# Softmax over rows on one core: three stores of 32 rows per partition in place of six of 16, and the scaling dealt out anew

## The chip, the core and the metric

The kernel runs on one core of one Trainium2 chip. The metric is the device time of one execution in microseconds. Before the change it is 160.23 us, the median of three runs (160.09 to 160.33).

The engines that matter here: VectorE (DVE in the profile), ScalarE (ACT), GpSimd (POOL), and SyncE (SP), which computes nothing and issues every transfer. The transfers run on 16 DMA engines, all fed through SP's one hardware queue.

## The reference

```python
def reference(x):                       # x: 16 x 1024 x 512, float32
    x_max = np.max(x, axis=-1, keepdims=True)
    exp_x = np.exp(x - x_max)
    return (exp_x / np.sum(exp_x, axis=-1, keepdims=True)).astype(np.float32)
```

There are 16,384 rows of 512 numbers, 2 KB each. 33.6 MB have to be read and as many written.

## The kernel before

The rows are flattened to 16,384 and cut into eight chunks of 4 MB. Each of the 128 partitions holds 16 successive rows of a chunk, so 32 KB lie together per partition both in DRAM and on the chip. The buffer `held` (line 79) has six places of 16 rows per partition. Chunks 6 and 7 therefore go into the places of chunks 0 and 1, once those have been stored. Everything is done in place: load, exponential, scaling, store.

Compute goes by groups of 8 rows per partition, two to a chunk, 16 in all. A group passes through four steps:

- M: `reduce_max` on VectorE (line 133) writes the negated row maxima into `shift`.
- exp: eight activations on ScalarE (line 165), one per row of the group, write the exponential in place and the row's sum into `sums`.
- the reciprocal of the sums on VectorE (line 142).
- the scaling, one `tensor_mul` of 128 x 4096 numbers with the reciprocals broadcast (line 144). It runs on VectorE for groups 12 to 15 (`ON_VECTOR`) and on GpSimd for the others. In the text, P5 is the scaling of group 5 on GpSimd, V14 that of group 14 on VectorE, M14 and exp 14 the other steps.

Each engine works through its instructions in the order in which they are written, and waits at semaphores. `take` (line 92) waits until a semaphore has reached a number and subtracts it. Four orders, written out by hand, make the schedule.

SP's order is the list `ORDER`: loads 0 to 5, stores 0, 1, 2, loads 6 and 7, stores 3 to 7. The first six loads wait for nothing (line 112), and the first of these is moved ahead of the start barrier by `loads_at_the_head`. A store waits for both scalings of its chunk, and load 6 or 7 waits until store 0 or 1 has landed:

```python
if what == "L":
    ...
        take(nc.sync, stored[k - PLACES], 16)
        ...
    nc.sync.dma_start(out=place(k), in_=x_rows[k]).then_inc(loaded[k], 16)
else:
    take(nc.sync, scaled[k], PER)
    nc.sync.dma_start(out=out_rows[k], in_=place(k)).then_inc(stored[k], 16)
```

VectorE's order is M0, M1, then by turns the reciprocal of group g - 1 (with its scaling, where that is VectorE's) and M of group g + 1, up to the scaling of group 15. The first M of a chunk waits for the chunk's load. ScalarE runs two loops with the same body, twelve turns for groups 0 to 11 and four for groups 12 to 15, because the second starts again at the first place of `held`. A turn waits for one count of `maxed`. GpSimd runs its twelve scalings in the order of the groups.

Of the kernel before, what the change touches and what calls it, by code (L numbers as in the profile page):

```python
# [1 line left out]

# [4 lines left out]

F32 = mybir.dt.float32
EXP = mybir.ActivationFunctionType.Exp
AX = mybir.AxisListType.X  # L10

CHUNK = 16
CHUNKS = 8
PLACES = 6
GROUP = 8
PER = CHUNK // GROUP
GROUPS = CHUNKS * PER
RING = PLACES * PER  # L20


ORDER = [("L", k) for k in range(PLACES)] + [
    ("S", 0),
    ("S", 1),
    ("S", 2),
    ("L", 6),
    ("L", 7),
    ("S", 3),
    ("S", 4),  # L30
    ("S", 5),
    ("S", 6),
    ("S", 7),
]


ON_VECTOR = (12, 13, 14, 15)


AT_HEAD = {mybir.EngineType.SP: 1}  # L40

def loads_at_the_head(nc):

    main, body = nc.main_func.blocks[0], nc.main_func.blocks[1]
    for engine, count in AT_HEAD.items():
        loads = [
            i
            for i in body.instructions  # L50
            if i.engine == engine and type(i).__name__ == "InstDMACopy"
        ][:count]
        barrier = next(
            n
            for n, i in enumerate(main.instructions)
            if i.engine == engine and type(i).__name__ == "InstDrain"
        )
        for load in loads:
            body.instructions.remove(load)
        main.instructions[barrier:barrier] = loads  # L60


@with_exitstack
def kernel(
    ctx: ExitStack,
    tc: tile.TileContext,
    x: bass.AP,
    out: bass.AP,
):
    nc = tc.nc  # L70
    nc.at_finalize(loads_at_the_head)
    P = nc.NUM_PARTITIONS

    x_rows = x.flatten_outer_dims().rearrange("(c p r) d -> c p r d", p=P, r=CHUNK)
    out_rows = out.flatten_outer_dims().rearrange("(c p r) d -> c p r d", p=P, r=CHUNK)
    n, _, _, d = x_rows.shape
    assert n == CHUNKS

    held = nc.alloc_sbuf_tensor("held", [P, PLACES * CHUNK, d], F32).ap()
    shift = nc.alloc_sbuf_tensor("shift", [P, GROUPS * GROUP], F32).ap()  # L80
    sums = nc.alloc_sbuf_tensor("sums", [P, GROUPS * GROUP], F32).ap()
    recip = nc.alloc_sbuf_tensor("recip", [P, GROUPS * GROUP], F32).ap()

    loaded = [nc.alloc_semaphore(f"loaded{k}") for k in range(CHUNKS)]
    stored = [nc.alloc_semaphore(f"stored{k}") for k in range(CHUNKS)]
    maxed = nc.alloc_semaphore("maxed")
    expd = nc.alloc_semaphore("expd")
    to_pool = nc.alloc_semaphore("to_pool")
    to_vector = nc.alloc_semaphore("to_vector")
    scaled = [nc.alloc_semaphore(f"scaled{k}") for k in range(CHUNKS)]  # L90

    def take(engine, semaphore, n):

        engine.wait_ge(semaphore, n).then_inc(semaphore, -n)  # L94

    def place(k):
        at = (k % PLACES) * CHUNK
        return held[:, at : at + CHUNK, :]

    def rows(g):  # L100
        at = (g % RING) * GROUP
        return held[:, at : at + GROUP, :]

    def stats(t, g):
        return t[:, g * GROUP : (g + 1) * GROUP]

    with tc.manual_schedule():  # L110
        for _, k in ORDER[:PLACES]:
            first = nc.sync.dma_start(out=place(k), in_=x_rows[k])
            first.then_inc(loaded[k], 16)
            tc.no_tile_sem_insts.add(first.ins.name)
    tc.close()
    tc.compile()  # L116

    reused = set()
    for what, k in ORDER[PLACES:]:
        if what == "L":  # L120
            if k >= PLACES:
                take(nc.sync, stored[k - PLACES], 16)
                reused.add(k - PLACES)
            nc.sync.dma_start(out=place(k), in_=x_rows[k]).then_inc(loaded[k], 16)
        else:
            take(nc.sync, scaled[k], PER)
            nc.sync.dma_start(out=out_rows[k], in_=place(k)).then_inc(stored[k], 16)


    def rowmax(g):  # L130
        if g % PER == 0:
            take(nc.vector, loaded[g // PER], 16)
        nc.vector.reduce_max(  # L133
            out=stats(shift, g), in_=rows(g), axis=AX, negate=True
        ).then_inc(maxed, 1)

    def scale(g):
        engine, ready = (
            (nc.vector, to_vector) if g in ON_VECTOR else (nc.gpsimd, to_pool)
        )  # L140
        take(nc.vector, expd, 1)
        nc.vector.reciprocal(out=stats(recip, g), in_=stats(sums, g)).then_inc(ready, 1)  # L142
        take(engine, ready, 1)
        engine.tensor_mul(  # L144
            out=rows(g),
            in0=rows(g),
            in1=stats(recip, g).unsqueeze(2).to_broadcast([P, GROUP, d]),
        ).then_inc(scaled[g // PER], 1)

    for g in range(GROUPS):  # L150
        rowmax(g)
        if g:
            scale(g - 1)
    scale(GROUPS - 1)


    nc.scalar.preload_act_table(EXP)  # L157

    def exps(first, turns):
        with nc.scalar.Fori(0, turns) as i:  # L160
            take(nc.scalar, maxed, 1)
            for r in range(GROUP):
                row = held[:, bass.ds(i * GROUP + r, 1), :]
                at = bass.ds(i * GROUP + (first * GROUP + r), 1)
                act = nc.scalar.activation(  # L165
                    out=row,
                    in_=row,
                    func=EXP,
                    bias=shift[:, at],
                    scale=1.0,  # L170
                    accum_out=sums[:, at],
                )
            act.then_inc(expd, 1)

    exps(0, RING)
    exps(RING, GROUPS - RING)


    for k in range(CHUNKS):
        if k not in reused:  # L180
            take(nc.sync, stored[k], 16)


# [1 line left out]
_INS = ['x']  # L185
_OUTS = [((16, 1024, 512), 'float32')]


# [23 lines left out]
```

## Time and profile before

| | before |
|---|---|
| median of three runs | 160.23 us (160.09 to 160.33) |
| the profiled execution | 160.32 us |
| its span, first to last instruction | 159.0 us |
| moved | 67.13 MB in 2306 packets, 422 GB/s over the span |
| busy: VectorE, ScalarE, GpSimd | 90.6, 92.0, 84.0 us |
| one reduction, one GpSimd scaling, one VectorE scaling (means) | 4.40, 7.02, 4.58 us |
| one activation (mean) | 0.706 us |
| loads, stores | 8 and 8, of 4 MB each |

The profile's page first gives the busy time of each engine, then the span in 40 equal slices, where each digit is the busy share in tenths and the DMA row is the mean share of the 16 DMA engines. After that come the share of the hardware queue, the chain of work that ended last, and the groups of instructions with busy time and mean duration. Beyond the page, the trace can be asked for the instructions of one engine in order of time: start, busy time, engine and line, operation, output and input, count, and in brackets the idle time before with what ended it. For one tile it gives the issues of its transfers in a window, with the duration and start of the issue and the time from issue to landing, each as minimum, median and maximum. All times are microseconds from the start of the span, durations of instructions in such rows nanoseconds.

### The profile page before, as it was taken

Reading aid. Unit: us, or ns where it says so; the run is one execution under the profiler, and the core shown is the slowest. Engines: PE = TensorE matmul, PEld = TensorE weight load, DVE = VectorE, ACT = ScalarE, POOL = GpSimd, SP = SyncE. Lnnn points to the kernel's source line nnn. Section 1 sums busy time; section 2 is a strip of 40 time slices with the busy share of each in tenths; the row PEclk is TensorE's granted clock in tenths of the full one; section 3 lists DMA queues with packets and bytes.
Section 4 is the critical chain, followed back from the end, with each engine's and each line's share of the span. In section 5 each row is a group of like instructions: output and inputs, shape, how many; then the busy total and the mean of one; then the engine's idle time right before and its main releaser. Section 6 shows DMA issues by size and latency. Waiting matters only on the chain. (4 is left out here: it accounts for less than half of the span.)

```text
span 159.0 us, 740 instructions
## 1 busy us (share of the span) xinstructions
DVE 90.6 (57%) x36; ACT 92.0 (58%) x257; POOL 84.0 (53%) x16
## 2 busy tenths in 40 slices
DVE  0008959777977977887700000695999998740000
ACT  0300699999999999999993000059934929200000
POOL 0000009999999999999999999259200000000000
DMA  7999999999999999999999999999999999999995
GB/s 264 470 445 404 404 478 437 396 470 445 404 404 470 445 396 396 396 412 470 437 396 445 470 404 404 478 437 398 437 437 437 412 462 414 437 437 429 429 429 256
DMA packets 2306, 67.13 MB, mean 422 GB/s; under 512 B 256, under 2 KB 256, under 8 KB 256
## 3 DMA queue, kind: packets, MB, share of 16 engines
q1 hardware_dynamic: 2304, 67.11, 98.8%
q14 instruction: 2, 0.02, 0.0%
HBM read 33.55 MB, written 33.55 MB: 422 GB/s over the span
## 5 line engine op out<-in xcount | busy, mean ns | idle before, releaser
L165 ACT ACTIVATE held<-held,shift x128 | 90.3, 706 | 40.0 <-ACTq L94 40.0
L144 POOL TENSOR_TENSOR held<-held,recip 128x4096 f32<-128x4096 f32 x12 | 83.8, 7018 | 28.1 <-POOLq L94 28.1
L133 DVE TENSOR_REDUCE shift<-held 128x8 f32<-128x4096 f32 x16 | 70.3, 4398 | 33.3 <-DVEq L94 33.3
L165 ACT ACTIVATION_READ_ACCUMULATOR held<-held,shift x128 | 23.8, 186 | 0.0
L144 DVE TENSOR_TENSOR held<-held,recip 128x4096 f32<-128x4096 f32 x4 | 18.3, 4576 | 0.6
L142 DVE RECIPROCAL recip<-sums 128x8 f32<-128x8 f32 x16 | 3.2, 201 | 16.4 <-DVEq L94 16.4
L157 ACT ACT_TABLE_LOAD x1 | 1.3, 1283 | 4.0 <-PEq L116 4.0
L196 POOL MEMSET const-float32-0.0<- 128x1 f32 x1 | 0.1, 99 | 0.2 <-issue 0.2
L196 POOL MEMSET const-uint8-127<- 128x1 uint8 x1 | 0.1, 103 | 0.0
L196 POOL MEMSET const-bfloat16-1.0<- 128x1 bf16 x1 | 0.1, 102 | 0.0
L196 POOL MEMSET const-float32-1.0<- 128x1 f32 x1 | 0.1, 99 | 0.0
## 6 DMA issues: line engine op xcount, KB each, us to landing
held<-in_x_dram SPq DMA_DIRECT2D x8, 4096.0 KB, 29.9
out_dram<-held SPq DMA_DIRECT2D x8, 4096.0 KB, 28.3
```

The costliest lines, as they stand in the source:

```text
L133: nc.vector.reduce_max(out=stats(shift, g), in_=rows(g), axis=AX, negate=True).then_inc(maxed, 1)
L142: nc.vector.reciprocal(out=stats(recip, g), in_=stats(sums, g)).then_inc(ready, 1)
L144: engine.tensor_mul(out=rows(g), in0=rows(g), in1=stats(recip, g).unsqueeze(2).to_broadcast([P, GROUP, d]),).then_inc(scaled[g // PER], 1)
L157: nc.scalar.preload_act_table(EXP)
L165: act = nc.scalar.activation(out=row, in_=row, func=EXP, bias=shift[:, at], scale=1.0, accum_out=sums[:, at],)
L196: nc = _bacc.Bacc("TRN2", target_bir_lowering=False, num_devices=1)
```

## The change

The unit is no longer a chunk but a range of rows per partition, of 128 in all. The first two ranges are laid out in DRAM as before, (0,16) and (16,32); the rest in three blocks of 32 rows per partition, so that 64 KB lie together per partition. Loads still bring 16 rows per partition each, now out of a 64 KB stretch from row 32 on. The stores of the three blocks send 32 rows per partition at once, 8 MB each. In SP's order the store of rows 32 to 63 stands ahead of the two late loads. Each store waits for the scaling of each of its groups, now two or four, each with a semaphore of its own.

VectorE's order is written out as a list. M is a reduction; P and V are both the reciprocal, followed by the scaling on GpSimd or on VectorE. GpSimd has 13 scalings instead of 12, and VectorE keeps three, of groups 7, 14 and 15. ScalarE has one loop of 16 turns, in which the place in `held` is the turn's remainder by 12.

```diff
-ORDER = [("L", k) for k in range(PLACES)] + [
-    ("S", 0),
-    ("S", 1),
-    ("S", 2),
-    ("L", 6),
-    ("L", 7),
-    ("S", 3),
-    ("S", 4),
-    ("S", 5),
-    ("S", 6),
-    ("S", 7),
+BLOCKS = [(0, 16), (16, 32), (32, 64), (64, 96), (96, 128)]
+ORDER = [
+    ("L", (0, 16)),
+    ("L", (16, 32)),
+    ("L", (32, 48)),
+    ("L", (48, 64)),
+    ("L", (64, 80)),
+    ("L", (80, 96)),
+    ("S", (0, 16)),
+    ("S", (16, 32)),
+    ("S", (32, 64)),
+    ("L", (96, 112)),
+    ("L", (112, 128)),
+    ("S", (64, 96)),
+    ("S", (96, 128)),
 ]
-ON_VECTOR = (12, 13, 14, 15)
+VECTOR = """
+    M0 M1 P0 M2 P1 M3 P2 M4 P3 M5 P4 M6 P5 M7 P6 M8 V7 M9 P8 M10 P9 M11
+    P10 P11 M12 M13 P12 M14 P13 M15 V14 V15
+"""
...
+    def in_dram(rows, a, b):
+        first, last = next(k for k in BLOCKS if k[0] <= a and b <= k[1])
+        block = rows[first * P : last * P].rearrange("(p r) d -> p r d", p=P)
+        return block[:, a - first : b - first, :]
...
-    for what, k in ORDER[PLACES:]:
+    for what, k in ORDER[AHEAD:]:
         if what == "L":
-            if k >= PLACES:
-                take(nc.sync, stored[k - PLACES], 16)
-                reused.add(k - PLACES)
-            nc.sync.dma_start(out=place(k), in_=x_rows[k]).then_inc(loaded[k], 16)
+            for s in stores:
+                if meets(s, k[0] - RING, k[1] - RING) and s not in taken:
+                    take(nc.sync, stored[s], 16)
+                    taken.add(s)
+            load(k)
         else:
-            take(nc.sync, scaled[k], PER)
-            nc.sync.dma_start(out=out_rows[k], in_=place(k)).then_inc(stored[k], 16)
+            for g in range(GROUPS):
+                if meets(k, *group(g)) and g not in done:
+                    take(nc.sync, scaled[g], 1)
+                    done.add(g)
+            nc.sync.dma_start(out=in_dram(out_rows, *k), in_=rows(*k)).then_inc(
+                stored[k], 16
+            )
...
-    for g in range(GROUPS):
-        rowmax(g)
-        if g:
-            scale(g - 1)
-    scale(GROUPS - 1)
+    for step in VECTOR.split():
+        what, g = step[0], int(step[1:])
+        if what == "M":
+            rowmax(g)
+        elif what == "V":
+            scale(g, nc.vector, to_vector)
+        else:
+            scale(g, nc.gpsimd, to_pool)
...
-        with nc.scalar.Fori(0, turns) as i:
+    with nc.scalar.Fori(0, GROUPS) as i:
...
-                row = held[:, bass.ds(i * GROUP + r, 1), :]
-                at = bass.ds(i * GROUP + (first * GROUP + r), 1)
+            row = held[:, bass.ds(i % (RING // GROUP) * GROUP + r, 1), :]
+            at = bass.ds(i * GROUP + r, 1)
...
-    exps(0, RING)
-    exps(RING, GROUPS - RING)
```

## The prediction

> **What bounds the kernel now.** I read the page first, for what is full, then the landing times of the transfers, then the engines' timelines around the last two loads.
>
> The page, the DMA row of the 40 slices and the row of the one hardware queue:
>
> ```profile
> DVE  0008959777977977887700000695999998740000
> ACT  0300699999999999999993000059934929200000
> POOL 0000009999999999999999999259200000000000
> DMA  7999999999999999999999999999999999999995
> ...
> q1 hardware_dynamic: 2304, 67.11, 98.8%
> ```
>
> The 16 DMA engines are full in every slice but the first and the last, while no compute engine is above 58%. 98.8% of 159.0 us is 157.1 us of transfers; the 1.9 us left are start and tail. So the end is set by the bytes, as long as the queue never runs dry. The question for any change is whether it does.
>
> Next, when each transfer lands (its tile's rows, one window for each issue; the first pair is the first load, then the two late loads, then the last store):
>
> ```profile
> L112 SPq DMA_DIRECT2D held<-in_x_dram x1: 383/383/383, 0.0 to 0.0; - x1
> ...
> DMA to landing us min/median/max: 12.3/12.3/12.3
> ...
> L124 SPq DMA_DIRECT2D held<-in_x_dram x1: 340/340/340, 71.3 to 71.3; - x1
> ...
> DMA to landing us min/median/max: 29.2/29.2/29.2
> ...
> L124 SPq DMA_DIRECT2D held<-in_x_dram x1: 339/339/339, 81.0 to 81.0; - x1
> ...
> DMA to landing us min/median/max: 29.3/29.3/29.3
> ...
> L127 SPq DMA_DIRECT2D out_dram<-held x1: 332/332/332, 141.0 to 141.0; - x1
> ...
> DMA to landing us min/median/max: 17.9/17.9/17.9
> ```
>
> Issue plus time to landing gives 12.3 for load 0, 100.5 for load 6, 110.3 for load 7, 158.9 for store 7. The other rows of the same kind give 61.5 for load 5, then 71.2, 81.0 and 90.8 for stores 0 to 2, and 120.1, 129.8, 139.6 and 149.3 for stores 3 to 6. Everything lands in the order of issue, 9.6 to 9.8 us apart: (158.9 - 12.3) / 15 = **9.77 us for 4 MB**. I use 9.75. The first load met an idle queue and took 12.3, so a transfer that finds the queue empty costs **2.55 us** more than its bytes. Data of the last store ends at 157.2 (the DMA share by microsecond falls there from 1.14 to 0.23), 1.7 before its landing, so a store must have data flowing 1.7 us before the one ahead of it lands. By the bytes moved up to 3.0 us (721 KB, 1.7 us at the mean rate) the first data flows 1.3 us after issue. Together: **a store must be issued 3.0 us before the one ahead lands**, or the queue runs dry. Store 7 was issued at 141.0 and needed by 149.3 - 3.0 = 146.3: a slack of 5.3 us.
>
> **The change, part by part.**
>
> *Order and size on the queue.* The bytes are the same. Stores (0,16) and (16,32) are issued as now (37.7, 51.6) and land at 71.2 and 81.0. Rows 32 to 63 go out as one store of 8 MB ahead of the late loads, two transfers where one stood (store 2): it lands at 81.0 + 19.5 = 100.5, the late loads at 110.25 and 120.0, each 9.75 later than now. Store (64,96) lands at 139.5. Store (96,128), now also 8 MB, needs its issue by 139.5 - 3.0 = **136.5**, 9.8 earlier than store 7 now. Three fewer transfers: the share above leaves no idle time between transfers, so I take nothing; the ends are from a loss to a gain of 0.4 (three times the 0.13 by which the pitch of 9.77 differs from its fastest, about 9.64). That 64 KB lie together per partition in a store, and that late loads step over 64 KB in DRAM, has no row here; 9.75 per 4 MB is the nearest, and I keep 1 us to either side for it.
>
> *Can store (32,64) go out in time?* It needs groups 4 to 7, by 81.0 - 3.0 = 78.0. GpSimd's eleven scalings start at 23.56 and run without a pause (76.77 / 11 = 6.98 each):
>
> ```profile
> 23.56 76.77 POOL L144 TENSOR_TENSOR held<-held,recip 128x4096 f32<-128x4096 f32 x11 [23.12 <-POOLq L94]
> 105.31 7.02 POOL L144 TENSOR_TENSOR held<-held,recip 128x4096 f32<-128x4096 f32 x1 [4.99 <-POOLq L94]
> ```
>
> Groups 0 to 6 on GpSimd end at 23.56 + 7 x 6.98 = 72.4. Group 7 goes to VectorE and could start at 62.9 (its reciprocal is at 62.61 now). But the trace shows what a VectorE scaling does beside a GpSimd one:
>
> ```profile
> 111.58 5.03 DVE L144 TENSOR_TENSOR held<-held,recip 128x4096 f32<-128x4096 f32 x1
> 116.53 4.41 DVE L133 TENSOR_REDUCE shift<-held 128x8 f32<-128x4096 f32 x1
> 120.86 0.18 DVE L142 RECIPROCAL recip<-sums 128x8 f32<-128x8 f32 x1
> 121.19 4.42 DVE L144 TENSOR_TENSOR held<-held,recip 128x4096 f32<-128x4096 f32 x1
> ```
>
> The first one began 0.75 us before GpSimd's last scaling ended (112.33) and took 5.03; the three others met an idle GpSimd and took 4.42. So 0.61 of the 0.75 shared microseconds were lost: while GpSimd scales, VectorE's two-tensor multiply almost stands still. The reductions (4.37 to 4.42 beside GpSimd, 4.41 without) lose nothing. The Trainium skill says the same more strictly ("SBUF — State Buffer", section "SBUF: two separate sides"): the pair of ports that the two engines share is locked for a whole instruction by whichever starts first, and the other blocks fully. By it the 5.03 would be 5.17; the trace is within 0.14 of that.
>
> Whichever goes first, then, the eight scalings follow each other: 72.4 + 4.4 = 76.8, store issued at **77.0**, 1.0 ahead of need. No gap, but thin. If they ran side by side it would be 72.5. Behind the waiting multiply on VectorE stand M9, and P8 to P11; at worst M9 starts at 76.9 instead of 62.7, ScalarE idles meanwhile, and GpSimd runs P8 to P11 from about 81.7 to 109.7. Store (64,96) is needed by 120.0 - 3.0 = 117.0, so this costs nothing. On SP the loads behind the store are issued at about 77.4 and 81.1, far ahead of their turn.
>
> *ScalarE's single loop.* It computes its row address with a remainder; per activation there are two fused register instructions where the first loop had one and an add. The old second loop already had two, and its activations at 105.33, 106.05, 106.76 and 107.46 keep the 0.705 pitch. I cost it at nothing; activations hide it up to 0.7 us per row.
>
> *The end of the chain.* All of it now hangs on load 6, landing at 110.25; M12 starts at 110.35 (100.60 now). With the same distances as now:
> M12 and M13 end at 114.8 and 119.2; exp 12 starts 4.73 after M12 starts (105.33 - 100.60), at 115.1, and exp 13 ends at 126.5. Reciprocal 12 comes 10.63 after M12's start, at 121.0. M14 stands behind it on VectorE, so it runs 121.1 to 125.5 although its load landed at 120.0. P12 on GpSimd starts 0.46 after its reciprocal (as 23.10 to 23.56), 121.4, and ends at 128.5; P13 follows to **135.4**. Reciprocal 13 at 126.5, M15 126.7 to 131.1. Exp 14 follows exp 13 (8 x 0.7055 = 5.64) to 132.1, exp 15 to 137.8. V14 is ready at 132.1 + 0.4 = 132.5, while GpSimd is in P13. If it stands still until 135.4 it ends at 135.4 + 4.3 = 139.7 (4.3, as 112.33 to 116.61); reciprocal 15, then V15 from 140.0 to **144.4**. If the two don't disturb each other, V14 ends at 137.0, V15 starts at 138.2 after exp 15 and ends at 142.6.
>
> SP issues the last store 0.1 later (140.92 to 141.01 now): 144.5, against a need at 136.5. The queue is dry, so the store pays in full: 12.3 + 9.75 = 22.05. It lands at 166.55, and the span ends 0.1 later: **166.65**, 7.65 over 159.0. The profiled execution took 160.32 for its span of 159.0, so 1.32 lie around it, and the median of the runs shown is 0.09 below that execution: 166.65 + 1.32 - 0.09 = **167.9 us**. In short: the last store becomes twice as long, so it must start 9.75 earlier, and its last load lands 9.75 later; 5.3 of slack and a faster finish from load to last scaling (24.4 against 30.6) don't pay for it.
>
> **The rivals.**
> 1. *No standing still of VectorE beside GpSimd* (V14 ends at 137.0): issue 142.7, span 164.85, time 166.1. The 5.03 row speaks against it.
> 2. *Store (32,64) misses its turn.* The cover is 1.0 us. If GpSimd and VectorE lose more than that over group 7, say 2 to 3, the queue is dry by 1 to 2, load 6 is as much later, and all behind it: 169 to 170. The thin margin is for it; against it, that no order of the two gives more than 76.8.
> 3. *The remainder in the loop costs more than the activation hides.* At 0.8 us a row, exp 15 ends at 115.1 + 32 x 0.8 = 140.7, later than V14: V15 then comes 1.1 later than summed, 169.0. At 0.9 it is another 3.2, and exp 7 at 74.8 (17.2 + 64 x 0.9) makes store (32,64) miss as well: 173 to 174. Against it, the pitch of the old second loop.
> 4. *Faster: larger runs move quicker.* The end hangs on the two 8 MB stores ahead of load 6 and at the end, 39 us together. To end before 159.0 they must save 7.7 of it, a rate 1.25 times today's, some 535 GB/s, from which on the change wins; at 1.3 times it gives 158.9. The stretches of 8 to 20 us that I read between 10 and 150 us show 416 to 449 GB/s. The Trainium skill ("DMA: Bandwidth & Descriptors", "Bandwidth") puts the fabric's ceiling at 435 GB/s, which excludes it; the 429 of the pitch agrees.
>
> **How the numbers follow.** Forecast (V14 stands still, no gap earlier) 0.70, 167.9. Rival 1 0.14, rival 2 0.09, rival 3 0.04, rival 4 0.03. The forecast's own bounds are 1 us to either side for the long runs and the idle start, 166.9 to 168.9; the range takes in rival 1 with a margin and the near end of rival 2: 165.6 to 169.3. About 0.2% is what a measurement of this kernel can tell from no change. Faster by more than that 0.02, within it 0.01, slower 0.97.
>
> **What would show it.** Right: GB/s near zero for 5 to 8 us at about 138 to 146; the last store issued near 144.5 and landing 22 us later; the late loads landing near 110 and 120; V14 longer than 6 us, ending 4.3 after P13. Wrong: V14 at 4.4 beside P13 (rival 1); a dip in GB/s near 80 (rival 2); an activation pitch over 0.71 (rival 3); landings less than 18 us apart for an 8 MB store (rival 4). No dip at 138 at all would undo the whole sum.

## The result, and the profile after

The changed kernel takes **166.62 us** (median of five runs, 166.27 to 166.69) against 160.21 us for the kernel before (median of five as well, 160.09 to 160.33): a ratio of 1.0395 with a 95% interval of 1.0383 to 1.0407, slower by 6.4 us. The forecast was 167.9 with a range of 165.6 to 169.3. The profiled span is 165.3 us, 6.3 more than before.

The page of the changed kernel, the rows that answer to those of before:

```profile
DVE  0009957977797788999550000029867789900000
ACT  0200899999999999409999000001999993000000
POOL 0000039999999999999999999200069970000000
DMA  7989999899999989899999969999989991099595
...
q1 hardware_dynamic: 1872, 67.11, 95.1%
```

The transfers fill 95.1% of 165.3 us, which is 157.2, as much as before (157.1). No byte became dearer; the queue had a hole. It stands in slices 34 and 35 of the DMA row (1 and 0). A slice is 4.13 us wide; the issues and landings bound the hole more closely. Rows of the changed kernel's transfers, issue and then time to landing; the two late loads, the store of rows 64 to 95, the last store:

```profile
L123 SPq DMA_DIRECT2D held<-in_x_dram x1: 630/630/630, 77.1 to 77.1; - x1
DMA to landing us min/median/max: 33.2/33.2/33.2
...
L123 SPq DMA_DIRECT2D held<-in_x_dram x1: 340/340/340, 81.1 to 81.1; - x1
DMA to landing us min/median/max: 39.0/39.0/39.0
...
L149 SPq DMA_DIRECT2D out_dram<-held x1: 344/344/344, 104.5 to 104.5; - x1
DMA to landing us min/median/max: 35.3/35.3/35.3
...
L149 SPq DMA_DIRECT2D out_dram<-held x1: 344/344/344, 144.5 to 144.5; - x1
DMA to landing us min/median/max: 20.7/20.7/20.7
```

Rows 0 to 95 are all stored at 139.8 (before: 139.6, store 5). The rest takes 25.4 us now and took 19.3 (158.9 - 139.6). So 6.1 of the 6.3 us lie behind that point. The last store was issued 4.7 us *after* the one ahead had landed, and it took 20.7 us, 1.4 more than the same 8 MB took before. Three windows of the changed kernel (window, length, busy time of each engine, clock, DMA share, GB/s) show what ran in the hole:

```profile
136.00:138.00 2.00, 2.00 (x1) 1.88 (x6) 0.00 (x0) 1.00 0.76 328
138.00:144.90 6.90, 6.29 (x3) 0.00 (x0) 0.00 (x0) 1.00 0.00 1
144.90:165.30 20.40, 0.00 (x0) 0.00 (x0) 0.00 (x0) 1.00 0.95 411
```

Only VectorE works between 138 and 144.9, and no packet of a load or store starts (the 1 GB/s is one packet of 8 KB of the queue that the page calls `instruction`). Its timeline, start and busy time first, shows with what: the first two rows are V7 and the reduction behind it, the last three V14, the reciprocal of group 15 and V15.

```profile
62.82 6.79 DVE L169 TENSOR_TENSOR held<-held,recip 128x4096 f32<-128x4096 f32 x1
69.53 4.41 DVE L161 TENSOR_REDUCE shift<-held 128x8 f32<-128x4096 f32 x1
...
133.14 6.61 DVE L169 TENSOR_TENSOR held<-held,recip 128x4096 f32<-128x4096 f32 x1 [0.56 <-DVEq L107]
139.68 0.19 DVE L167 RECIPROCAL recip<-sums 128x8 f32<-128x8 f32 x1
140.01 4.43 DVE L169 TENSOR_TENSOR held<-held,recip 128x4096 f32<-128x4096 f32 x1
```

GpSimd's timeline has P12 and P13 back to back, to 135.47, and of P6 in its own window (duration in nanoseconds, start) this:

```profile
121.48 13.99 POOL L169 TENSOR_TENSOR held<-held,recip 128x4096 f32<-128x4096 f32 x2 [17.10 <-POOLq L107]
...
L169 POOL TENSOR_TENSOR held<-held,recip x1: 11199/11199/11199, 65.3 to 65.3; 128x4096 f32<-128x4096 f32 x1
```

V14 began at 133.14 and ended at 139.75, 4.28 after P13: it stood still for 2.2 us. V7 met P5, waited until 65.3, and then ran, and P6 waited for it: 11.2 us in place of 7.0. A wait for the other engine thus shows as a longer instruction, not as idle time.

ScalarE's rows of the single loop keep the pitch of the old second loop, 0.70 to 0.72 us (start, busy time; the read of the sum between them left out), and the mean of all 128 is 0.708 against 0.706:

```profile
115.20 0.72 ACT L192 ACTIVATE held<-held,shift  x1 [23.88 <-ACTq L107]
...
115.92 0.71 ACT L192 ACTIVATE held<-held,shift  x1
...
116.62 0.71 ACT L192 ACTIVATE held<-held,shift  x1
```

### The profile page after: what moved, and what is told of

It reads as the page before. It is cut to its first block, busy times and chain, and to the rows that moved or that the text cites. A ratio compares the mean times of both kernels' runs of the same rounds, so it can differ in the third digit from the quotient of the medians.

```text
span 165.3 us, 741 instructions
## 1 busy us (share of the span) xinstructions
DVE 90.2 (55%) x35; ACT 91.9 (56%) x257; POOL 95.1 (58%) x17
## 3 DMA queue, kind: packets, MB, share of 16 engines
q1 hardware_dynamic: 1872, 67.11, 95.1%
## 5 line engine op out<-in xcount | busy, mean ns | idle before, releaser
L169 POOL TENSOR_TENSOR held<-held,recip 128x4096 f32<-128x4096 f32 x13 | 94.9, 7336 | 40.1 <-POOLq L107 40.1
L169 DVE TENSOR_TENSOR held<-held,recip 128x4096 f32<-128x4096 f32 x3 | 17.8, 5942 | 0.9 <-DVEq L107 0.6
```

The lines of the kernel that those rows point to most:

```text
L169: engine.tensor_mul(out=rows(*group(g)), in0=rows(*group(g)), in1=stats(recip, g).unsqueeze(2).to_broadcast([P, GROUP, d]),).then_inc(scal ...
```

## The experiments

Two theories were to be told apart. **A**: transfers move at the old rate, and the time is lost because the last 8 MB store has to wait for the last scaling and finds the queue dry. **B**: the larger stores, the loads that step over 64 KB, or the place of a store ahead of the loads make transfers slower in themselves. Beside it stood the sizes: what a dry queue costs, and how early a store must be issued.

### The last store cut in two

```diff
-    ("S", (96, 128)),
+    ("S", (96, 112)),
+    ("S", (112, 128)),
```

> The last store is cut in two, rows 96 to 111 (groups 12 and 13) and 112 to 127 (14 and 15); all else as in the changed kernel. Theory A (the 8 MB store waits for the last scaling, and the queue runs dry for 6 us): the first half is issued when GpSimd's scaling 13 ends, at 135.5 by the changed kernel's trace, ahead of the landing at 139.8; the second at 144.5, ahead of the first half's landing at about 149.5. No gap, span 158.9 to 159.2, time 160.2 (160.0 to 160.5), some 6.4 under the changed kernel. Theory B (the larger stores, the 64 KB step of the loads, or the place of the store ahead of the loads make transfers slower in themselves): two of the three large stores and the place remain, so at least half of the loss stays: 163 or more.

Measured: 160.17 us, a ratio of 1.0005 to the kernel before (0.9996 to 1.0014), span 158.8. The whole loss is gone, with two large stores, their place and the stepping loads left in. The windows of this run, where the changed kernel had its hole:

```profile
134.00:138.00 4.00, 4.00 (x1) 3.63 (x12) 1.20 (x1) 1.00 0.68 295
138.00:142.00 4.00, 3.85 (x3) 0.00 (x0) 0.00 (x0) 1.00 1.00 428
142.00:146.00 4.00, 2.17 (x1) 0.00 (x0) 0.00 (x0) 1.00 1.06 459
```

VectorE does the same work at the same time, but the first half (groups 12 and 13) was issued at 135.3 and covers it. Theory B falls.

### The late loads ahead of the store of rows 32 to 63

```diff
-    ("S", (32, 64)),
     ("L", (96, 112)),
     ("L", (112, 128)),
+    ("S", (32, 64)),
```

> The three 8 MB stores stay, but the store of rows 32 to 63 goes behind the two late loads again. Theory A: the late loads land near 90.8 and 100.5, the last scaling ends near 127.5, and the last 8 MB store is issued some 10 us before its turn at 138. No gap; span 158.5 to 159.1, time 159.8 to 160.3: the size of the stores costs nothing by itself, and saves at most 0.4 by three fewer transfers. Theory B: the large stores cost by themselves, so that 163 or more remain.

Measured: 160.10 us, ratio 0.9997 (0.9988 to 1.0007), span 158.9. The last 8 MB store was issued at 127.6 and landed 31.3 later:

```profile
L149 SPq DMA_DIRECT2D out_dram<-held x1: 332/332/332, 127.6 to 127.6; - x1
DMA to landing us min/median/max: 31.3/31.3/31.3
```

So three stores of 8 MB cost nothing by themselves, and the three transfers that are saved bring nothing that the measurement can see. It is the combination that costs: a last store twice as long, behind loads moved back by as much.

### Group 7 scaled by GpSimd

```diff
-    M0 M1 P0 M2 P1 M3 P2 M4 P3 M5 P4 M6 P5 M7 P6 M8 V7 M9 P8 M10 P9 M11
+    M0 M1 P0 M2 P1 M3 P2 M4 P3 M5 P4 M6 P5 M7 P6 M8 P7 M9 P8 M10 P9 M11
```

> Group 7 is scaled by GpSimd, so no VectorE scaling stands beside GpSimd's there; GpSimd ends group 7 at 23.4 + 8 x 6.98 = 79.3 and the store of rows 32 to 63 is issued at 79.4 instead of 76.65. If a store must be issued 3.0 us before the one ahead of it lands (81.0), as predicted, the queue is dry for 1.4 us and everything behind it is later: 168.0. If the need is shorter, as the changed kernel's last store suggests (issued at 144.5, landed 20.7 later, so only 1.3 over two times 9.75), it needs its issue by 79.7 and nothing changes: 166.6 (166.3 to 166.9).

Measured: 167.36 us (ratio to the kernel before 1.046, 1.0444 to 1.0476), span 165.9: between the two. The store of rows 32 to 63:

```profile
L149 SPq DMA_DIRECT2D out_dram<-held x1: 332/332/332, 79.5 to 79.5; - x1
DMA to landing us min/median/max: 21.7/21.7/21.7
```

It lands at 101.2, against 76.65 + 24.0 = 100.65 in the changed kernel: half a microsecond late, though issued 1.6 ahead of the landing before it (81.1). So an issue 1.6 ahead costs half a microsecond here, and the changed kernel's 4.3 ahead costs none; what lies between was not measured.

The trace also keeps each packet, and these show that the queue hardly ran dry. The transfer ahead ends on the 16 DMA engines at 80.11 to 80.64. The store's first packets start at 80.31 to 80.65, the earliest 0.84 after the issue, and on average an engine waits 0.02 us. An estimate from these figures is that no engine waits when the issue lies 0.84 + (81.08 - 80.11), some 1.8 us, ahead of the landing. The half microsecond is lost at the store's end: its last packet on each engine takes 2.8 to 3.5 us, against 2.4 to 2.5 in the changed kernel, though loads follow it there too. Why a store that was issued late ends like this is not shown.

### A load that meets a dry queue

```diff
-                if meets(s, k[0] - RING, k[1] - RING) and s not in taken:
+                if s not in taken and (
+                    meets(s, k[0] - RING, k[1] - RING)
+                    or (k == (96, 112) and s == (32, 64))
+                ):
```

> Load 6 also waits until the store of rows 32 to 63 has landed, so it meets an idle queue in the middle of the run. If an idle queue costs 2.55 us over the pitch wherever it occurs, as predicted from the first load, load 6 lands 12.3 after its issue and all behind it is 2.65 later: 169.2. If the first load's excess belongs to the start of the program and an idle queue costs 1.25, as the changed kernel's last store suggests, load 6 lands 11.0 after issue and the time is 168.0. A third outcome, that loads have the long excess and stores the short one, looks like the first here and is told from it by a cold store of 16 rows.

Measured: 168.84 us (ratio 1.054, 1.0524 to 1.0556), span 167.6, 2.3 more than the changed kernel. The load's row, then that of the last store in the same run:

```profile
L123 SPq DMA_DIRECT2D held<-in_x_dram x1: 340/340/340, 100.6 to 100.6; - x1
DMA to landing us min/median/max: 12.0/12.0/12.0
...
L152 SPq DMA_DIRECT2D out_dram<-held x1: 344/344/344, 146.8 to 146.8; - x1
DMA to landing us min/median/max: 20.7/20.7/20.7
```

A load on a dry queue takes 12.0 in mid-run, nearly the 12.3 at the start: 2.25 over the pitch of 9.75. The start of the program is not the cause. The last store again pays only 1.2 (20.7 less twice 9.75).

### Two cold stores of 16 rows

The last block goes out as two stores, and the first waits for the groups of both.

```diff
-    ("S", (96, 128)),
+    ("S", (96, 112)),
+    ("S", (112, 128)),
...
-                if meets(k, *group(g)) and g not in done:
+                due = meets(k, *group(g)) or (k == (96, 112) and g > 13)
+                if due and g not in done:
```

> The last block goes out as two stores of 16 rows, but both wait for all four of its groups, so a 4 MB store meets the idle queue at 144.5 and the other follows it. If what the idle queue costs hangs on the direction (loads 12.3 and 12.0 from issue to landing, a store less), the first lands 10.9 to 11.1 after issue, the second 20.6 to 20.9 after the first's issue, and the time is that of the changed kernel, 166.6 (166.3 to 167.0). If the 64 KB runs of the 8 MB store made its 20.7, these stores of 32 KB runs pay as the loads do: 12.0 to 12.3 and 21.8 to 22.1, time 167.8.

Measured: 166.59 us, span 165.0. The window of both issues gives both landings as minimum and maximum:

```profile
L151 SPq DMA_DIRECT2D out_dram<-held x2: 343/384/425, 144.1 to 144.5; - x2
DMA to landing us min/median/max: 11.2/15.8/20.5
```

A cold store of 4 MB lands 11.2 us after issue, a cold load of the same size 12.0 to 12.3. The direction sets the price, not the length of the runs: the two halves, with 32 KB per packet, are through 20.9 us after the first issue, and the one store with 64 KB took 20.7. The packets in the traces show where: the first packet on an engine takes 1.2 us in this store and 1.8 on average in the cold load of the run before, and the first of all starts 0.85 us after the issue here and 0.97 there.

### The old deal of the scalings

VectorE's list as the loop before had it, the rest as in the changed kernel:

```diff
-    M0 M1 P0 M2 P1 M3 P2 M4 P3 M5 P4 M6 P5 M7 P6 M8 V7 M9 P8 M10 P9 M11
-    P10 P11 M12 M13 P12 M14 P13 M15 V14 V15
+    M0 M1 P0 M2 P1 M3 P2 M4 P3 M5 P4 M6 P5 M7 P6 M8 P7 M9 P8 M10 P9 M11
+    P10 M12 P11 M13 V12 M14 V13 M15 V14 V15
```

> Stores, their order and the single loop as in the changed kernel, but VectorE's order and the dealing out of the scalings as before the change: groups 12 to 15 on VectorE, group 7 on GpSimd, P11 behind M12. By the sum of the prediction: store (32,64) as in the run with group 7 on GpSimd (79.5), load 6 lands at 110.9; P11 waits for M12 and ends at 122.8, so store (64,96) is issued at 122.9, after the landing of load 7 near 120.7; on VectorE four scalings stand between and behind the reductions, V15 ends near 151.3, and the last store lands 20.7 later: span 172.2, time 173.5 (172.5 to 174.5). If the new deal has no part in the result, the time is that of the run with group 7 on GpSimd, 167.4.

Measured: 173.98 us (ratio 1.0852, 1.0824 to 1.088), span 172.5. V15 on VectorE's timeline, and the last store:

```profile
147.24 4.42 DVE L169 TENSOR_TENSOR held<-held,recip 128x4096 f32<-128x4096 f32 x1
...
L149 SPq DMA_DIRECT2D out_dram<-held x1: 343/343/343, 151.8 to 151.8; - x1
DMA to landing us min/median/max: 20.7/20.7/20.7
```

The new deal is worth 7.4 us with these stores: it takes back more than half of the 13.8 that they would cost with the old one.

### No scaling of group 13

```diff
-        nc.vector.reciprocal(out=stats(recip, g), in_=stats(sums, g)).then_inc(ready, 1)
+        inverse = nc.vector.reciprocal(out=stats(recip, g), in_=stats(sums, g))
+        if g == 13:
+            inverse.then_inc(scaled[g], 1)
+            return
+        inverse.then_inc(ready, 1)
```

> The scaling of group 13 on GpSimd is left out (its rows are stored unscaled; the reciprocal reports the group as done), so GpSimd is idle when V14 is ready. If V14 stands still beside P13 in the changed kernel, it now takes 4.42 from about 132.7, V15 starts when exp 15 is through, at 138.2, the last store is issued at 142.7 and the time is 1.8 less, 164.8 (164.5 to 165.1). If V14's 6.6 has another cause, V14 stays at 6.6 and the time at 166.6.

Measured: 164.81 us (ratio 1.0274, 1.0252 to 1.0295), span 163.7, 1.8 less in the time. Group 13 stays unscaled. The same V14 and V15, now with GpSimd idle from 128.5 on:

```profile
133.14 4.42 DVE L173 TENSOR_TENSOR held<-held,recip 128x4096 f32<-128x4096 f32 x1 [0.56 <-DVEq L107]
...
138.37 4.43 DVE L173 TENSOR_TENSOR held<-held,recip 128x4096 f32<-128x4096 f32 x1
```

V14 starts at the same 133.14 and takes 4.42 in place of 6.61. P13 was what held it.

### What makes a cold store dearer

In the run with the old deal a cold 8 MB store in mid-run landed 21.9 us after issue, the last one 20.7:

```profile
L149 SPq DMA_DIRECT2D out_dram<-held x1: 344/344/344, 123.1 to 123.1; - x1
DMA to landing us min/median/max: 21.9/21.9/21.9
```

First, VectorE kept busy beside the cold last store:

```diff
+    spare = nc.alloc_sbuf_tensor("spare", [P, 6, d], F32).ap()
...
+    for n in range(6):
+        nc.vector.tensor_mul(out=spare[:, n, :], in0=held[:, 16, :], in1=held[:, 17, :])
```

> The changed kernel with six more multiplications of 128 x 512 on VectorE behind V15, into a buffer that nothing reads, so that VectorE is busy for some 3.5 us while the last store meets the idle queue. A cold 8 MB store took 20.7 from issue to landing where no engine computed beside it, and 21.9 in the run with the old deal, where VectorE was scaling and a load had gone before. If the busy VectorE makes the 1.2 more, the last store now lands 21.9 after issue, span 166.5; if what went before makes it, 20.7 and 165.3 remain.

Measured: landing 20.8 us after issue, span 165.0, time 166.43. VectorE was busy from 144.00 to 147.69, while the store started, and made no difference:

```profile
144.00 3.69 DVE L185 TENSOR_TENSOR spare<-held 128x512 f32<-128x512 f32 x6
...
L150 SPq DMA_DIRECT2D out_dram<-held x1: 343/343/343, 144.2 to 144.2; - x1
DMA to landing us min/median/max: 20.8/20.8/20.8
```

Second, the store of rows 64 to 95 ahead of the late loads:

```diff
     ("S", (32, 64)),
+    ("S", (64, 96)),
     ("L", (96, 112)),
     ("L", (112, 128)),
-    ("S", (64, 96)),
```

> The store of rows 64 to 95 goes ahead of the late loads as well, so the last store meets a queue that last moved loads, with no engine computing beside it. Loads 6 and 7 land near 130 and 139.7, V15 ends some 24.4 later, near 164.1, and the store is issued then. If a store behind loads pays more, it lands 21.9 after issue, span 186.2; if only a busy VectorE makes that, 20.7, span 185.0. Either way the time is about 186 to 188, some 20 over the changed kernel: by the theory of the dry queue each 8 MB that goes ahead of the late loads costs another 19.5.

Measured: span 191.1, time 192.5, far over the 186 to 188 expected. Its expectation forgot that the moved store needs groups 8 to 11, scaled at 104.5. The rows of this run, that store and then the last:

```profile
L149 SPq DMA_DIRECT2D out_dram<-held x1: 333/333/333, 104.6 to 104.6; - x1
DMA to landing us min/median/max: 21.7/21.7/21.7
...
L149 SPq DMA_DIRECT2D out_dram<-held x1: 343/343/343, 170.3 to 170.3; - x1
DMA to landing us min/median/max: 20.7/20.7/20.7
```

It is issued 4.3 us after the store ahead had landed (100.3), and lands 6.5 later than without a gap (100.3 + 19.5 = 119.8, and 126.3); both late loads stand behind it on SP and in the queue and are later still. The last store, now behind loads, takes 20.7 all the same. So neither a busy VectorE nor the direction of the transfer ahead makes the extra 1.0 to 1.2 of the mid-run stores (21.7, 21.9). The length of the dry time does not either: the last stores came 3.4 us (without the scaling of group 13) to 24.5 us (this run) after the landing ahead, and all took 20.7 or 20.8.

The packets and the completion signals in the two traces show that the two stores lost their time in different ways. In the run with the old deal 15 of the 16 DMA engines report the end 20.6 to 20.75 us after the issue, exactly as with the last stores. Only the 16th reports at 21.9. The store closes there at 144.01, when a packet of 8 KB of the `instruction` queue (143.71 to 144.02) ends; that this packet held it up is the likely reading, but the trace does not name the engines. In the run just shown all 16 report late, 21.2 to 21.7 after the issue, because the last packet on each takes 2.9 to 3.5 us in place of 2.4, as in the store of rows 32 to 63 with group 7 on GpSimd. In both of these a load follows the late store, and behind the last stores there is nothing. What makes the packets longer stays open. It does not touch the verdict, because the last store took 20.7 or 20.8 wherever it was cold.

## Why the prediction held, and where it was off

*The order on the queue* was right to 0.3 us: late loads forecast at 110.25 and 120.0, landed at 110.3 and 120.1; store (64,96) forecast at 139.5, landed at 139.8. Taking nothing for three fewer transfers and for the 64 KB runs was right too: 0.9997 with the large stores in a harmless order.

*Store (32,64)* was forecast for 77.0 and issued at 76.65, in time. The two engines excluded each other as said, with VectorE first. That its cover was thin is shown by giving group 7 to GpSimd: 2.8 us later cost 0.7 us of the time.

*ScalarE's loop* cost nothing, as the pitch shows.

*The end of the chain*: V15 was forecast for 140.0 to 144.4 and ran 140.01 to 144.44, the store forecast for 144.5 and issued then. V14 started 0.6 later than summed: its row has 0.56 us of idle time in front, which the trace names only as a wait of the engine's queue. P13 covered that. That V14 stood still beside P13 was worth 1.8 us in the sum and 1.8 when P13 was left out. With it rival 1 falls. By the lock of the Trainium skill ("SBUF — State Buffer", section "SBUF: two separate sides") the second engine waits for the end of the first; V14 ending 4.28 after P13, within 0.14 of the 4.42 that it takes alone, and P6's 11.2 us behind V7, agree with it.

*The step that was off* is "the queue is dry, so the store pays in full: 12.3 + 9.75 = 22.05". It took 20.7, and these 1.35 us are the whole error (166.65 - 165.3 in the span). The 12.3 was a load's time; a store on a dry queue pays 1.2 to 1.5 over the pitch here, a load 2.25 to 2.55. The same trace also held a misreading. "Data of the last store ends at 157.2, 1.7 before its landing" took the microsecond windows as if a packet's time lay where it is spent. In the changed kernel windows read 2.43 and then 0.00 by turns, more than all engines can do in one microsecond. A packet is counted where it starts, and the packets of the trace say how far that misleads: in the kernel before the last ones start at 157.3 and take 1.2 us, so the data end at 158.5, 0.5 before the landing. The misreading made the needed lead 3.0 us; the run with group 7 on GpSimd puts it at some 1.8, by the estimate given there. In the kernel before, store 7 would by that have had some 6.5 us of slack, not 5.3. The forecast of the end did not depend on it, because the last store came far too late by either figure.

Rivals 2 to 4 fall too: there was no gap at 80 (the store of rows 32 to 63 landed 19.65 after the one ahead, at 100.65 and 81.0), the pitch of the activations stayed at 0.70 to 0.72, and 8 MB in 19.65 are no faster than before.

None of the versions that were run beats the kernel before beyond the measurement. The two that are level with it (1.0005 and 0.9997) repair the changed kernel in one edit each.

## What to carry to other kernels

Where a transfer queue is full from end to end, merging transfers saves only their seams, here nothing that could be measured, while each merge makes the transfer wait for its last part and the next wait for the whole. So before merging, write down for each transfer when its last producer ends and when the queue reaches it: the last one here needed its data 10 us earlier than before, and its last load came 10 us later. And a scaling given to GpSimd is not parallel to one on VectorE: read a longer duration, not idle time, as the sign that the two are waiting for each other.

## What the runs showed of the hardware that was not expected

- A store to a dry queue is cheaper than a load: 4 MB land 11.2 us after issue against 12.0 to 12.3, and 8 MB in 20.7.
- A store that was issued late and has a load behind it can end slowly: its last packets of 64 KB took 2.8 to 3.5 us in place of 2.4, and it landed 0.5 to 1.0 later. Why is open.
- 64 KB that lie together per partition go out as one packet each (1872 packets, of which three stores give 128 each, ten transfers 128 each and all thirteen 16 small ones), and move no faster than 32 KB: three transfers of 8 MB and ten of 4 MB end at 158.9, like sixteen of 4 MB at 159.0.
- VectorE's waiting multiplication got its turn at the end of GpSimd's current scaling although the next one was ready: P6 waited and took 11.2 us.
